# Two output projections as 2x2 block products with seven products in place of eight

## The chip, the cores and the metric

The kernel runs on one NeuronCore of one Trainium2 chip, as one program. The metric is the device time of one execution in microseconds; the times shown are of three executions.

## The reference

Two encoder layers are computed for 64 sample tokens (of a running stream) and 512 prompt tokens, 576 in all, with a model width of 2048. Layer A is attention over a band of chunks with 16 heads of 128; layer B is latent attention with 16 heads. Both end in the same way, and that end is what is changed:

```python
y = x + (jax.nn.silu(g) * o) @ w_out      # w_out: 2048 x 2048, once in a_prompt/a_sample, once in b_prompt/b_sample
```

`x` is the layer's input (for layer B the `y` of layer A), `o` the heads' outputs side by side (2048 columns), `g` a gate of the same width. Layer B begins with `rmsnorm(x) @ w_b_in`. All of it is float32.

## The kernel before, in words

All activations are kept transposed: features on the 128 partitions, the 576 tokens on the free axis, so a 2048x576 matrix is 16 tiles of 128x576. Weights are the stationary operand. A float32 product is three float32r passes: each operand is split into a rounded part `hi` (a cast on ACT) and the rest `lo` (a subtraction on DVE), and TensorE adds hi*hi, hi*lo and lo*hi into one PSUM sum.

An output projection goes over 16 output tiles `m`. For each, `proj` takes 16 tiles of input features (`o2`, hi and lo, which stay in SBUF), three passes each, with the 576 tokens in two halves of 288 that lie in two PSUM banks: 96 matmuls a tile. `wload` brings a quarter of a tile's weights (128x512, 256 KB) by the SP queue into one of three raw buffers and splits it into one of five pairs of hi and lo buffers; `Weights` does that three quarters ahead. The first two output tiles (`both`) are merged with the last heads of attention: their matmuls fill the time in which PE would wait for a head. Tile by tile DVE then adds the residual (L681 in layer A, L1039 in layer B). In layer A the sum `x1` goes to DRAM (`x1d`, by the POOL queue; layer B reads it again as its residual) and is split in SBUF at once, with the factor per feature of layer B's norm (`split_g`, L686), into `h`, the operand of layer B's input products (`lat`). Its squares are summed for the norm (L265).

In layer B attention has no room for the heads' outputs in SBUF; 14 of 16 go to DRAM (`od`) and are read back and split in time (`reload`); the last two are split from SBUF.

The order of PE's instructions is the program's: class `Order` merges streams (attention, gates, output) into one fixed list, in which a stream waits for a time, a PSUM buffer or a condition. The other engines and queues are ordered by the framework's scheduler from priorities and dependences, each again as one fixed list that its engine goes through in order; it also sets the semaphore waits. PSUM has a tag `mm` of two tiles of two banks, and one tile each of `st` and `x`.

Of the kernel before, what the change touches and what calls it, by code (L numbers as in the profile page):

```python
# [12 lines left out]
F32 = mybir.dt.float32  # L13
F32R = mybir.dt.float32r
# [75 lines left out]
class Weights:  # L90
    """Tiles of weights in the order of their use, each loaded and split `ahead` of it."""
# [24 lines left out]
def encoder(tc, xT, wa_in, wa_out, wb_in, wuq, wuk, wuqr, wuv, wb_out, kcT, vc, ckvcT, krcT, gains, rtab,  # L116
# [38 lines left out]
    def matmul(out, lhs, rhs, start, stop):  # L155
# [5 lines left out]
        nc.tensor.matmul(out, lhs, rhs, start=start, stop=stop)  # L161
# [95 lines left out]

    def square_sum(acc, src, tp, w, first, name):
        """acc += src**2, elementwise."""
# [7 lines left out]
    def col_sums(sq, tp, w, ones_ap, name, wait=2.0):  # L267
        """st[:, c, :w/2] = column sums of sq on every partition; and two buffers that are free then."""
# [12 lines left out]
    def halves(src, tp, w, name):  # L281
        """The column sums of src**2: the squares of both halves of the partitions are added first."""
# [57 lines left out]
    def gate(ps, rs, dst, tp, name):  # L340
        """dst = silu(ps * rs), the sigmoid as exp(min(g, 0) - ln(1 + exp(-|g|)))."""
# [9 lines left out]
    def softmax(s_ps, w, nb, pp, name):  # L351
        """Rows of exp(-(s + nb)) over their sum, s the negated scores."""
# [96 lines left out]
    # ------------------------------------------------------------------ layer A: input  # L449
# [42 lines left out]
    def head_a(hd):  # L492
        """The projections of a head; what follows each goes its own way."""
# [67 lines left out]
        def bias():  # L561
            """By relative position, less its value at far keys; negated."""
# [84 lines left out]
    wo = Weights(wload, two_first(parts_of(wa_out, range(KT), "wao")), 3)  # L647
# [10 lines left out]
    # ------------------------------------------------------------------ layer A: output  # L658
    close(g_at)
    close(g_o)  # L660
    g_x1, x1p = pool("x1", side="right")
    g_ao, aop = pool("aout", side="right")

    def tpo(tag, dt, name):
        return aop.tile([P, N], dt, tag=tag, bufs=2 if tag in ("xr", "x1", "s1") else 1, name=name)

    h = []
    acc = tpo("acc", F32, "lnb_acc")

    def out_a():  # L670
        for m in range(KT):
            xr = tpo("xr", F32, f"xr{m}")
            nc.sync.dma_start(xr, xT[m * P:(m + 1) * P, :])
            if m < 2:
                ps = first[m]
            else:
                yield "mm"
                ps = ps_of("mm", f"ao{m}")
                yield from proj(ps, wo, o2, N)
            x1 = tpo("x1", F32, f"x1_{m}")  # L680
            V.tensor_tensor(out=two(x1), in0=ps[:, :, :288], in1=two(xr), op=ALU.add)  # L681
            od_.give("mm", L_M)
            nc.gpsimd.dma_start(x1d[m * P:(m + 1) * P, :], x1)
            hi = x1p.tile([P, N], F32R, tag="x1", bufs=32, name=f"bh{m}")
            lo = x1p.tile([P, N], F32R, tag="x1", bufs=32, name=f"bl{m}")
            split_g(x1, gn[:, G_LNB + m:G_LNB + m + 1], hi, lo)  # L686
            h.append((hi, lo))
            square_sum(acc, x1, tpo, N, m == 0, f"lnb{m}")
# [5 lines left out]
    # ------------------------------------------------------------------ layer B: latents  # L694
# [6 lines left out]
    close(g_ao)  # L701
    g_l, lp = pool("lat")
# [4 lines left out]

    cq = [(lp.tile([P, N], F32R, name=f"cqh{m}"), lp.tile([P, N], F32R, name=f"cql{m}")) for m in range(4)]
# [20 lines left out]
    def rope(x, name):  # L729
        """x rotated in place; x: two stacked sets of 64 features."""  # L730
# [44 lines left out]
    def rotary_key(ps):  # L775
        """Twice: rows 64.. repeat rows ..63."""
# [26 lines left out]
    def queries():  # L803
        """Of the heads, rotary ones two heads at a time; to DRAM."""
# [47 lines left out]
    # ------------------------------------------------------------------ layer B: heads  # L852
# [23 lines left out]
    def prepare():  # L876
        """Keys of the heads, values of two at a time."""
# [16 lines left out]
    def values_of(pr, w):  # L894
        """Of two heads, tokens on partitions."""
# [37 lines left out]
    def fetch():  # L933
        """The heads' queries."""
# [17 lines left out]
    def attend(hd):  # L952
# [25 lines left out]
        if hd < H - DIRECT:  # L978
            nc.gpsimd.dma_start(od[hd * P:(hd + 1) * P, :], sg)
        else:  # L980
# [25 lines left out]
    wo = Weights(wload, two_first(parts_of(wb_out, range(KT), "wbo")), 3)  # L1006
    first = []

    def out_first():
        """The first tiles of the output, as far as heads are done."""  # L1010
# [14 lines left out]
    # ------------------------------------------------------------------ layer B: output  # L1025
    g_bo, bo = pool("bout")

    def out_b():
        for m in range(KT):
            xr = bo.tile([P, N], F32, tag="xr", bufs=2, name=f"bxr{m}")  # L1030
            nc.sync.dma_start(xr, x1d[m * P:(m + 1) * P, :])
            if m < 2:
                ps = first[m]
            else:
                yield "mm"
                ps = ps_of("mm", f"bo{m}")
                yield from proj(ps, wo, o2, N)
            y = bo.tile([P, N], F32, tag="y", bufs=2, name=f"by{m}")
            V.tensor_tensor(out=two(y), in0=ps[:, :, :288], in1=two(xr), op=ALU.add)  # L1039
            od_.give("mm", L_M)  # L1040
            nc.gpsimd.dma_start(yT[m * P:(m + 1) * P, :], y)
# [99 lines left out]
```

## Time and profile before

| what | us |
|---|---|
| time, median of three executions | 2042.68 (2042.22 to 2042.9) |
| span of the profiled execution (its own time is recorded only as this span) | 2040.6 |
| TensorE (PE) busy | 2021.8 |
| VectorE (DVE) busy | 1182.7 |
| ScalarE (ACT) busy | 1037.9 |
| GpSimd (POOL) busy | 73.5 |
| layer A, output tiles 2 to 15: from, to | 974, 1153 |
| layer B, output tiles 2 to 15: from, to | 1856, 2035 |

The page gives busy times of one execution; a matmul's own duration overlaps with the next one's, so the time that one takes is read from the distance of two starts or from a piece of the chain, not from its mean duration. The same holds for DVE, where successive instructions overlap by some 0.09 us. PE's line says that it hardly ever rests. What another engine's time means is to be read stage by stage, from what PE waits for there.

### The profile page before, as it was taken

To read this page: it belongs to the slowest core of one execution; us is meant where nothing else is said; L and a number is where in the kernel's file an instruction comes from. 1 tells how busy PE (TensorE), PEld (TensorE's weight loads), DVE (VectorE), ACT (ScalarE), POOL (GpSimd) and SP (SyncE) were. 2 spreads that over 40 slices of the span, in tenths; PEclk is the share of its full clock that TensorE was granted. 3 is DMA by queue.
4 is the path that set the end of the run, shared out by engine and by line. 5 is a ranking of instruction groups with operands and counts; after the bars stand their busy time and mean duration, and the time that the engine had idled before them with its cause. 6 is when DMAs were issued, how large, how long until landed. Compare 5 with 4: busy or idle time off the path is not lost.

```text
span 2040.6 us, 37379 instructions
## 1 busy us (share of the span) xinstructions
PE 2021.8 (99%) x14980; PEld 2002.9 (98%) x14980; DVE 1182.7 (58%) x2295; ACT 1037.9 (51%) x1898; POOL 73.5 (4%) x139
## 2 busy tenths in 40 slices
PE   8999999999999999999999999999999999999998
PEld 8999999999999999999999999999999999999998
DVE  7665555555555555556433448887776766673221
ACT  6654444544454445455333338886765656572111
POOL 0000000000000000000000000000000000000000
PEclk9999999999999999999999999999999999999999
DMA  7333333333333332323444425563223322354442
GB/s 212 85 84 94 90 85 90 82 86 89 86 94 89 86 90 77 85 81 91 145 129 130 122 75 145 160 165 119 77 82 92 88 85 88 83 150 138 129 129 76
DMA packets 116621, 213.33 MB, mean 105 GB/s; under 512 B 13728, under 2 KB 28720, under 8 KB 116448
## 3 DMA queue, kind: packets, MB, share of 16 engines
q1 hardware_dynamic: 104752, 171.78, 31.0%
q0 software_dynamic: 11696, 39.17, 5.5%
q8 instruction: 117, 1.92, 0.4%
q14 instruction: 56, 0.46, 0.1%
HBM read 174.48 MB, written 33.77 MB: 102 GB/s over the span
## 4 chain that ended last, share of the span: by engine, by line
PE 89%; issue 8%; DVE 1%; ACT 1%; POOL 0%; DMA 0%; POOLq 0%; DVEq 0%; ACTq 0%
PE ao L161 10%; PE g L161 8%; PE lat L161 7%; PE u L161 3%; PE a2p L161 3%; PE bo L161 3%; PE a7p L161 3%; PE a15p L161 3%; PE a13p L161 3%; PE a10p L161 3%; PE a8p L161 3%; PE a12p L161 3%; PE a14p L161 3%; PE a6p L161 3%; PE a5p L161 3%
## 5 line engine op out<-in xcount | busy, mean ns | idle before, releaser
L201 DVE TENSOR_TENSOR wa_2l<-wa_2r,wa_2h 128x512 fp32r<-128x512 f32 x61 | 42.2, 691 | 92.2 <-ACT wa_2h L200 92.2
L200 ACT CAST wa_2h<-wa_2r 128x512 fp32r<-128x512 f32 x61 | 37.7, 619 | 103.7 <-PE a2p L161 10.1
L200 ACT CAST wa_0h<-wa_0r 128x512 fp32r<-128x512 f32 x61 | 37.8, 619 | 61.1 <-PE a2p L161 4.3
L201 DVE TENSOR_TENSOR wa_3l<-wa_3r,wa_3h 128x512 fp32r<-128x512 f32 x61 | 42.2, 692 | 43.5 <-ACT wa_3h L200 42.0
L200 ACT CAST wa_3h<-wa_3r 128x512 fp32r<-128x512 f32 x61 | 37.7, 618 | 50.8 <-PE a2p L161 4.5
L201 DVE TENSOR_TENSOR wa_0l<-wa_0r,wa_0h 128x512 fp32r<-128x512 f32 x61 | 41.9, 687 | 17.6 <-ACT wa_0h L200 17.6
L200 ACT CAST wa_1h<-wa_1r 128x512 fp32r<-128x512 f32 x61 | 37.8, 620 | 25.0 <-PE a0pg L161 2.6
L201 DVE TENSOR_TENSOR wa_1l<-wa_1r,wa_1h 128x512 fp32r<-128x512 f32 x61 | 41.8, 686 | 11.8 <-ACT wa_1h L200 11.7
L1039 DVE TENSOR_TENSOR by<-bo,bxr 128x576 f32<-128x576 f32 x16 | 12.1, 757 | 43.5 <-PE bo L161 43.5
L681 DVE TENSOR_TENSOR x<-ao,xr 128x576 f32<-128x576 f32 x16 | 12.1, 758 | 33.1 <-PE ao L161 33.1
L201 DVE TENSOR_TENSOR wao_3l<-wao_3r,wao_3h 128x512 fp32r<-128x512 f32 x16 | 11.1, 691 | 34.1 <-ACT wao_3h L200 34.1
L201 DVE TENSOR_TENSOR wbo_2l<-wbo_2r,wbo_2h 128x512 fp32r<-128x512 f32 x16 | 11.0, 690 | 32.9 <-ACT wbo_2h L200 32.9
L201 DVE TENSOR_TENSOR wbo_3l<-wbo_3r,wbo_3h 128x512 fp32r<-128x512 f32 x16 | 11.0, 690 | 32.7 <-ACT wbo_3h L200 32.6
L200 ACT CAST wao_3h<-wao_3r 128x512 fp32r<-128x512 f32 x16 | 9.9, 620 | 39.2 <-PE ao L161 39.2
L201 DVE TENSOR_TENSOR wao_2l<-wao_2r,wao_2h 128x512 fp32r<-128x512 f32 x16 | 11.1, 691 | 32.5 <-ACT wao_2h L200 32.3
L200 ACT CAST wbo_3h<-wbo_3r 128x512 fp32r<-128x512 f32 x16 | 9.9, 621 | 37.8 <-PE bo L161 37.7
L161 PE MATMUL u<-cqh,wq_0h 128*128 128x288 f32 x128 | 27.6, 297 | 0.5 <-ACT q6raw L336 0.3
L201 DVE TENSOR_TENSOR wb_1l<-wb_1r,wb_1h 128x512 fp32r<-128x512 f32 x25 | 17.2, 688 | 18.6 <-ACT wb_1h L200 18.6
L201 DVE TENSOR_TENSOR wbo_1l<-wbo_1r,wbo_1h 128x512 fp32r<-128x512 f32 x16 | 11.0, 690 | 29.1 <-ACT wbo_1h L200 29.1
L161 PE MATMUL ao<-oh,wao_1h 128*128 128x288 f32 x128 | 27.6, 297 | 0.0
L161 PE MATMUL ao<-oh,wao_0h 128*128 128x288 f32 x128 | 27.5, 296 | 0.0
L161 PE MATMUL bo<-boh,wbo_2h 128*128 128x288 f32 x128 | 27.5, 296 | 0.0
(5236 smaller groups left out, 7717.5 us busy)
## 6 DMA issues: line engine op xcount, KB each, us to landing
wa_0r<-wa_in SPq DMA_DIRECT2D x61, 256.0 KB, 2.9
wa_1r<-wa_in SPq DMA_DIRECT2D x61, 256.0 KB, 2.9
wa_2r<-wa_in SPq DMA_DIRECT2D x61, 256.0 KB, 2.9
wa_3r<-wa_in SPq DMA_DIRECT2D x61, 256.0 KB, 2.9
wb_0r<-wb_in SPq DMA_DIRECT2D x25, 256.0 KB, 3.0
wb_1r<-wb_in SPq DMA_DIRECT2D x25, 256.0 KB, 3.0
wb_2r<-wb_in SPq DMA_DIRECT2D x25, 256.0 KB, 3.0
wb_3r<-wb_in SPq DMA_DIRECT2D x25, 256.0 KB, 2.9
```

The costliest lines, as they stand in the source:

```text
L161: nc.tensor.matmul(out, lhs, rhs, start=start, stop=stop)
L200: ACT.copy(hi, src)
L201: V.tensor_tensor(out=lo, in0=src, in1=hi.bitcast(F32), op=ALU.subtract)
L681: V.tensor_tensor(out=two(x1), in0=ps[:, :, :288], in1=two(xr), op=ALU.add)
L1039: V.tensor_tensor(out=two(y), in0=ps[:, :, :288], in1=two(xr), op=ALU.add)
```

## The change

The first two output tiles of each layer are made as before. The other 14 are made as seven pairs. A pair of output tiles (256 features) by 576 tokens is cut into four quarters (a tile, a half of the tokens), and the 2048 input features into two halves of eight tiles: a 2x2 block product of 2x2 blocks, which takes eight block products of 24 matmuls. The new code takes seven, in Winograd's form of Strassen's scheme, over sums and differences of blocks:

- `block_operands` builds the four combined operands (numbers 4 to 7; 1 to 3 are parts of `o2`) once a layer, from the float32 outputs of the heads, in place, and splits them; number 4 is put where one half of `o2` was.
- `block_weights` loads a pair's eight raw blocks and builds its sums S0 and S1 and differences, on DVE (L324, 327, 330, 334), then splits 14 of them.
- `block_pairs` does the products. Those of five numbers accumulate on sums already in PSUM: a tile of two banks takes all products but number 2. After each product DVE adds what the bank holds to the output (L391).

In layer A the raw weights take the 16 buffers of the heads' outputs (`oA`). `x1` goes only to DRAM; when the projection's buffers are free, 16 loads (L855) bring it back for `split_g`. In layer B all 16 heads go to `od`, and after the heads' buffers are free 16 loads (`bf`, L1196) bring them back for `block_operands`; the raw weights then take the same 16 buffers.

```diff
+    def block_operands(o, o2, pool, name):
+        L, R = slice(0, 288), slice(288, 576)
+        ...                                  # X[1], X[2], X[3]: halves of o2
+        def put(p, j, src):
+            if p == 4:
+                hi, lo = [x[:, R] for x in o2[j]]
+            else:
+                hi = pool.tile([P, 288], F32R, tag="T", bufs=48, name=f"{name}T{p}h{j}")
+                lo = pool.tile([P, 288], F32R, tag="T", bufs=48, name=f"{name}T{p}l{j}")
+            split(src, hi, lo)
+            X[p].append((hi, lo))
+        for j in range(8):
+            V.tensor_tensor(out=o[j][:, L], in0=o[j][:, R], in1=o[j][:, L], op=sub)
+            put(5, j, o[j][:, L])
+        for j in range(8):
+            a, b = o[j], o[j + 8]
+            V.tensor_tensor(out=a[:, R], in0=b[:, R], in1=a[:, R], op=sub)
+            V.tensor_tensor(out=b[:, R], in0=b[:, R], in1=a[:, L], op=sub)
+            put(6, j, b[:, R])
+        ...                                  # 7 from o[j][:, R]; 4 from o[j+8][:, L] - o[j+8][:, R]
+    def block_weights(w2d, pairs, order, raw_tile, name):
+        ...
+                    elif p == 5:
+                        S[c] = raw_tile(f"{n_}s{c}")
+                        V.tensor_tensor(out=S[c], in0=block(1, 0, c), in1=block(1, 1, c), op=ALU.add)
+                    elif p == 6:
+                        V.tensor_tensor(out=S[c], in0=S[c], in1=block(0, 0, c), op=ALU.subtract)
+        ...
+                    split(src, hi, lo)
+                    yield hi, lo
+    def block_pairs(w2d, X, pairs, raw_tile, residual, out_tile, done, name):
+        order = [(1, 2, 5, 6, 3, 7, 4) if n == 0 else (1, 5, 6, 3, 7, 2, 4) for n in range(len(pairs))]
+        ws = Ahead(block_weights(w2d, pairs, order, raw_tile, name), WHL - 2)
+        for (m1, m2), seq in zip(pairs, order):
+            ...
+            ps = ps_of("mm", n_ + "ac")
+            bank = {1: ps[:, 0, :288], 5: ps[:, 1, :288]}
+            bank[6] = bank[7] = bank[4] = bank[1]
+            bank[3] = bank[5]
+            for p in seq:
+                if p == 2:
+                    bank[2] = ps_of("x", n_ + "b")[:, :288]
+                for c in range(2):
+                    hi, lo = ws.get()
+                    for j in range(4):
+                        ...
+                        begins = p in (1, 2, 5) and c == 0 and j == 0
+                        matmul(bank[p], hi[:, s], xh, begins, False, skip_group_check=True)
+                        matmul(bank[p], hi[:, s], xl, False, False, skip_group_check=True)
+                        matmul(bank[p], lo[:, s], xh, False, ends, skip_group_check=True)
+                with tc.high_priority():
+                    y, h_, add = ...
+                    V.tensor_tensor(out=y[:, h_], in0=bank[p], in1=add[:, h_], op=ALU.add)
@@ layer A
+    X = block_operands(oA, o2, Tp, "ao")
+    def raw_a(name):
+        return op_.tile([P, WH], F32, tag="o", bufs=16, name=name)
+    def done_a(m, x1):
+        nc.gpsimd.dma_start(x1d[m * P:(m + 1) * P, :], x1)
+        square_sum(acc, x1, tpo, N, m == 0, f"lnb{m}")
-            hi = x1p.tile([P, N], F32R, tag="x1", bufs=32, name=f"bh{m}")
-            lo = x1p.tile([P, N], F32R, tag="x1", bufs=32, name=f"bl{m}")
-            split_g(x1, gn[:, G_LNB + m:G_LNB + m + 1], hi, lo)
@@ layer B, latents
+    for m in range(KT):
+        x1 = tpl("raw", F32, f"bx{m}")
+        nc.sync.dma_start(x1, x1d[m * P:(m + 1) * P, :])
+        ...
+        split_g(x1, gn[:, G_LNB + m:G_LNB + m + 1], hi, lo)
@@ layer B, heads
-        if hd < H - DIRECT:
-            nc.gpsimd.dma_start(od[hd * P:(hd + 1) * P, :], sg)
-        else:
+        nc.gpsimd.dma_start(od[hd * P:(hd + 1) * P, :], sg)
+        if hd >= H - DIRECT:
@@ layer B, output
+    for kt in range(KT):
+        oB.append(bo.tile([P, N], F32, tag="o", bufs=16, name=f"bf{kt}"))
+        nc.sync.dma_start(oB[kt], od[kt * P:(kt + 1) * P, :])
+    X = block_operands(oB, o2, bo, "bo")
```

Three places in the engines' lists follow. First PE in layer A, where the sum that is made changes: before from output tile 8 (`ao8`) to tile 9, after from product 5 to product 6 of the pair of tiles 8 and 9 (`ao8p5...` and `ao8p6...` are the weights, `aoT5...` and `aoT6...` the combined operands). In brackets stands what a matmul waits for. Before:

```order
L161 MATMUL ao8_12074<-oh15_11203,wao8_3h_12076 128x288 x2
L161 MATMUL ao8_12074<-ol15_11204,wao8_3h_12076 128x288 x2
L161 MATMUL ao8_12074<-oh15_11203,wao8_3l_12077 128x288 x2
L161 MATMUL ao9_12207<-oh0_10861,wao9_0h_12106 128x288 [waits DVE_49,Activation_49]
L161 MATMUL ao9_12207<-oh0_10861,wao9_0h_12106 128x288
L161 MATMUL ao9_12207<-ol0_10862,wao9_0h_12106 128x288 x2
```

After:

```order
L164 MATMUL ao8ac_12238<-aoT5h7_11265,ao8p51h_12245 128x288
L164 MATMUL ao8ac_12238<-aoT5l7_11266,ao8p51h_12245 128x288
L164 MATMUL ao8ac_12238<-aoT5h7_11265,ao8p51l_12246 128x288
L164 MATMUL ao8ac_12238<-aoT6h0_11271,ao8p60h_12262 128x288 [waits DVE_49,Activation_49]
L164 MATMUL ao8ac_12238<-aoT6l0_11272,ao8p60h_12262 128x288
L164 MATMUL ao8ac_12238<-aoT6h0_11271,ao8p60l_12263 128x288
```

Before, the sum changes to another tile (`ao8`, `ao9`), and the wait on DVE is for an addition to a tile that was finished 96 matmuls earlier. After, both products are in one tile, `ao8ac`, in its two banks, and the count of DVE that product 6 waits for is that of the addition `x1_9<-ao8ac,xr9` (L391), which waits for product 5's last matmul.

The second place is DVE at the end of layer A's last head, from its last multiplication (`a15sg`) on. `ol` are lo parts of the heads' outputs, `wao` and `ao2p` weights. Before:

```order
L427 TENSOR_TENSOR a15sg_10850<-a15sg_10850,a15o3_11085 128x512
L201 TENSOR_TENSOR ol15_11204<-a15sg_10850,oh15_11203 128x576
L201 TENSOR_TENSOR wao2_1l_11181<-wao2_1r_11179,wao2_1h_11180 128x512
L201 TENSOR_TENSOR wao2_2l_11193<-wao2_2r_11191,wao2_2h_11192 128x512
L681 TENSOR_TENSOR x1_0_11254<-ao0_10859,xr0_11252 128x576
```

After, the first rows and the last:

```order
L567 TENSOR_TENSOR a15sg_10850<-a15sg_10850,a15o3_11085 128x512
L204 TENSOR_TENSOR aoT5l0_11231<-a0sg_769,aoT5h0_11230 128x288
L290 TENSOR_TENSOR a4sg_3547<-a12sg_8867,a4sg_3547 128x288
L204 TENSOR_TENSOR aoT5l1_11236<-a1sg_1540,aoT5h1_11235 128x288
L204 TENSOR_TENSOR ol15_11186<-a15sg_10850,oh15_11185 128x576
...
L204 TENSOR_TENSOR aoT7l7_11346<-a7sg_5542,aoT7h7_11345 128x288
L204 TENSOR_TENSOR ol7_11031<-a15sg_10850,oh7_11030 128x288
L825 TENSOR_TENSOR x1_1_11385<-ao1_10860,xr1_11383 128x576
L204 TENSOR_TENSOR ao2p10l_11401<-ao2r2_0_11398,ao2p10h_11400 128x512
```

The weights of output tile 2 stood two rows behind the multiplication; now 51 rows (48 of 288 columns, 3 of 576) stand between it and the first weights of the pair of tiles 2 and 3.

The third place is SP's queue of loads in layer B, behind the last head read back for the first two tiles (`bo13`). Before:

```order
L993 DMA bo13_21354<-od_70 128x576
L214 DMA wbo2_0r_21510<-wb_out 128x512
L214 DMA wbo2_1r_21576<-wb_out 128x512
L214 DMA wbo2_2r_21588<-wb_out 128x512
L214 DMA wbo2_3r_21654<-wb_out 128x512
L1031 DMA bxr0_21641<-x1d_69 128x576
```

After:

```order
L1144 DMA bo13_21640<-od_70 128x576
L1196 DMA bf0_21910<-od_70 128x576
L1196 DMA bf1_21912<-od_70 128x576
...
L1196 DMA bf14_21938<-od_70 128x576
L1196 DMA bf15_21940<-od_70 128x576
L1184 DMA bxr0_22086<-x1d_69 128x576
L1184 DMA bxr1_22091<-x1d_69 128x576
L309 DMA bo2r2_0_22103<-wb_out 128x512
```

The weights of tile 2 stood right behind `bo13`; now the 16 loads of the heads' outputs and two of the residual go first. The load of `bf1` takes the buffer of the last head's output and waits for that one's write to `od`.

## Rows read from the trace of the kernel before

**Rows 1.** The page: span, and busy time of each engine (share of the span, instructions).
```profile
span 2040.6 us, 37379 instructions
...
PE 2021.8 (99%) x14980; PEld 2002.9 (98%) x14980; DVE 1182.7 (58%) x2295; ACT 1037.9 (51%) x1898; POOL 73.5 (4%) x139
```

**Rows 2.** Chain of waits, two stretches: start us, us, what.
```profile
961.18 192.00 PE ao L161 x1440
...
1518.36 6.48 PE v3v L161 x54
```

**Rows 3.** By stretch: us, busy PE, PEld, DVE, ACT, POOL; clock, DMA share, GB/s.
```profile
974.00:1153.00 179.00, 179.00 (x1344) 179.00 (x1344) 69.52 (x99) 54.08 (x86) 7.58 (x15) 1.00 0.46 132
1856.00:2035.00 179.00, 179.00 (x1344) 178.90 (x1342) 45.30 (x66) 32.05 (x52) 7.58 (x14) 1.00 0.41 122
7.00:30.00 23.00, 22.68 (x153) 22.34 (x154) 18.56 (x28) 18.00 (x30) 0.00 (x0) 1.00 0.86 266
25.00:30.00 5.00, 5.00 (x39) 5.00 (x39) 2.86 (x6) 3.14 (x6) 0.00 (x0) 1.00 0.92 303
```

**Rows 4.** PE, timeline: start us, us, instruction xcount [idle before <-what ended it].
```profile
86.78 0.42 PE L161 MATMUL a1p<-hh,wa_2l 128*128 128x288 f32 x2
88.20 0.50 PE L161 MATMUL a10st<-a10s,ones 128*128 128x288 f32 x2 [1.00 <-DVE a01sq L325]
88.54 0.42 PE L161 MATMUL a1p<-hh,wa_3h 128*128 128x288 f32 x2
...
961.01 0.42 PE L161 MATMUL ao<-oh,wao_2h 128*128 128x288 f32 x2
...
1153.02 0.42 PE L161 MATMUL lat<-bh,wb_0h 128*128 128x288 f32 x2
...
1846.98 0.43 PE L161 MATMUL bo<-boh,wbo_2h 128*128 128x288 f32 x2
...
2034.71 0.42 PE L161 MATMUL bo<-boh,wbo_3l 128*128 128x288 f32 x2
```

**Rows 5.** DVE, timeline of the same places.
```profile
87.31 0.75 DVE L325 SCALAR_TENSOR_TENSOR a01sq<-a01st,a01sq 128x576 f32<-128x576 f32 x1
...
936.21 0.67 DVE L201 TENSOR_TENSOR wao_1l<-wao_1r,wao_1h 128x512 fp32r<-128x512 f32 x1
936.81 0.74 DVE L201 TENSOR_TENSOR ol<-a4sg,oh 128x576 fp32r<-128x576 f32 x1
...
941.36 0.75 DVE L201 TENSOR_TENSOR ol<-a8sg,oh 128x576 fp32r<-128x576 f32 x1
942.02 0.75 DVE L201 TENSOR_TENSOR ol<-a9sg,oh 128x576 fp32r<-128x576 f32 x1
...
961.22 0.69 DVE L427 TENSOR_TENSOR a15sg<-a15sg,a15o 128x512 f32<-128x512 f32 x1 [0.84 <-PE a15o L161]
...
1847.18 0.69 DVE L427 TENSOR_TENSOR g15sg<-g15sg,b15o 128x512 f32<-128x512 f32 x1 [3.82 <-PE b15o L161]
...
2035.17 0.76 DVE L1039 TENSOR_TENSOR by<-bo,bxr 128x576 f32<-128x576 f32 x1 [12.04 <-PE bo L161]
```

**Rows 6.** Groups, DVE, forms apart: instruction xcount | busy, mean ns | idle before.
```profile
L527 DVE TENSOR_TENSOR a0vt<-a0pv,rs 128x288 f32<-128x288 f32 x2 | 0.8, 451 | 0.0
```

**Rows 7.** DMA issues: out<-in, queue, KB each, median us to landing.
```profile
x1d<-x POOLq DMA_DIRECT2D x16, 288.0 KB, 3.9
...
wao_0r<-wa_out SPq DMA_DIRECT2D x16, 256.0 KB, 2.9
...
od<-g8sg POOLq DMA_DIRECT2D x1, 288.0 KB, 2.4
```

**Rows 8.** PE, timeline of the kernel's start.
```profile
8.81 0.68 PE L161 MATMUL a0pq<-hh,wa_0l 128*128 128x288 f32 x2
...
12.02 0.43 PE L161 MATMUL a0pg<-hh,wa_0h 128*128 128x288 f32 x2
```

More of the change, by code (lines that the diff above doesn't have):

```diff
@@ L153, in two, with matmul @@
         return ap.rearrange("p (c n) -> p c n", c=2)
-    def matmul(out, lhs, rhs, start, stop):
+    def matmul(out, lhs, rhs, start, stop, **kw):
         n = rhs.shape[-1]
@@ L160, in matmul @@
             od_.now += 4 * (n / 2.4 + 2) / 1e3
-        nc.tensor.matmul(out, lhs, rhs, start=start, stop=stop)
+        nc.tensor.matmul(out, lhs, rhs, start=start, stop=stop, **kw)
     def transpose(out, in_):
@@ new lines, in block_weights, with load, block @@
+    def block_weights(w2d, pairs, order, raw_tile, name):
+        for (m1, m2), seq in zip(pairs, order):
+            n_ = f"{name}{m1}"
+            got, S = {}, {}
+            def load(m, part):
+                r = raw_tile(f"{n_}r{m}_{part}")
+                nc.sync.dma_start(r, w2d[m * P:(m + 1) * P, part * WH:(part + 1) * WH])
+                return r
+            def block(i, k, c):
+                key = i, k, c
+                if key not in got:
+                    got[key] = load((m1, m2)[i], 2 * k + c)
+                return got[key]
+            for p in seq:
+                for c in range(2):
+                    if p == 1:
+                        src = block(0, 0, c)
+                    elif p == 5:
+                        S[c] = raw_tile(f"{n_}s{c}")
+                        V.tensor_tensor(out=S[c], in0=block(1, 0, c), in1=block(1, 1, c), op=ALU.add)
+                        src = S[c]
+                    elif p == 6:
+                        V.tensor_tensor(out=S[c], in0=S[c], in1=block(0, 0, c), op=ALU.subtract)
+                        src = S[c]
+                    elif p == 3:
+                        V.tensor_tensor(out=S[c], in0=block(0, 1, c), in1=S[c], op=ALU.subtract)
+                        src = S[c]
+                    elif p == 7:
+                        src = block(1, 0, c)
+                        V.tensor_tensor(out=src, in0=block(0, 0, c), in1=src, op=ALU.subtract)
+                    elif p == 2:
+                        src = block(0, 1, c)
+                    else:
+                        src = block(1, 1, c)
+                    hi = wp.tile([P, WH], F32R, tag="whi", bufs=WHL, name=f"{n_}p{p}{c}h")
+                    lo = wp.tile([P, WH], F32R, tag="wlo", bufs=WHL, name=f"{n_}p{p}{c}l")
+                    split(src, hi, lo)
+                    yield hi, lo
@@ new lines, in encoder, with __init__, fill, get @@
+    class Ahead:
+        def __init__(self, gen, n):
+            self.gen, self.n, self.got = gen, n, []
+        def fill(self, n):
+            while len(self.got) < n:
+                x = next(self.gen, None)
+                if x is None:
+                    break
+                self.got.append(x)
+        def get(self):
+            self.fill(self.n + 1)
+            return self.got.pop(0)
+    def block_pairs(w2d, X, pairs, raw_tile, residual, out_tile, done, name):
+        L, R = slice(0, 288), slice(288, 576)
+        order = [(1, 2, 5, 6, 3, 7, 4) if n == 0 else (1, 5, 6, 3, 7, 2, 4) for n in range(len(pairs))]
+        ws = Ahead(block_weights(w2d, pairs, order, raw_tile, name), WHL - 2)
+        for (m1, m2), seq in zip(pairs, order):
+            n_ = f"{name}{m1}"
+            x1, x2 = residual(m1), residual(m2)
+            y1, y2 = out_tile(m1), out_tile(m2)
+            yield "mm"
+            ps = ps_of("mm", n_ + "ac")
+            bank = {1: ps[:, 0, :288], 5: ps[:, 1, :288]}
+            bank[6] = bank[7] = bank[4] = bank[1]
+            bank[3] = bank[5]
+            for p in seq:
+                if p == 2:
+                    yield "x"
+                    bank[2] = ps_of("x", n_ + "b")[:, :288]
+                for c in range(2):
+                    hi, lo = ws.get()
+                    for j in range(4):
+                        s = slice(j * P, (j + 1) * P)
+                        xh, xl = X[p][4 * c + j]
+                        ends = c == 1 and j == 3
+                        begins = p in (1, 2, 5) and c == 0 and j == 0
+                        matmul(bank[p], hi[:, s], xh, begins, False, skip_group_check=True)
+                        matmul(bank[p], hi[:, s], xl, False, False, skip_group_check=True)
+                        matmul(bank[p], lo[:, s], xh, False, ends, skip_group_check=True)
+                        yield None
+                with tc.high_priority():
+                    y, h_, add = {1: (y1, L, x1), 5: (y2, R, x2), 6: (y1, R, x1), 3: (y1, R, y1), 7: (y2, R, y2),
+                                  2: (y1, L, y1), 4: (y2, L, x2)}[p]
+                    V.tensor_tensor(out=y[:, h_], in0=bank[p], in1=add[:, h_], op=ALU.add)
+                if p == 2:
+                    od_.give("x", L_M)
+            od_.give("mm", L_M)
+            done(m1, y1)
+            done(m2, y2)
@@ L645, in heads_a @@
                 o2[j] = hi, lo
-    wo = Weights(wload, two_first(parts_of(wa_out, range(KT), "wao")), 3)
+    wo = Weights(wload, two_first(parts_of(wa_out, range(2), "wao")), 3)
     first = []
@@ L701, in encoder @@
     close(g_ao)
+    close(g_T)
+    close(g_o)
+    g_x1, x1p = pool("x1", side="right")
     g_l, lp = pool("lat")
@@ L977, in attend @@
         sg = gates[hd][0]
-        if hd < H - DIRECT:
-            nc.gpsimd.dma_start(od[hd * P:(hd + 1) * P, :], sg)
-        else:
+        nc.gpsimd.dma_start(od[hd * P:(hd + 1) * P, :], sg)
+        if hd >= H - DIRECT:
             yield lambda: flag["gates"] == KT and o2[hd - 1] is not None
@@ L1004, in heads_in @@
         yield since[kt] + 4.0
-    wo = Weights(wload, two_first(parts_of(wb_out, range(KT), "wbo")), 3)
+    wo = Weights(wload, two_first(parts_of(wb_out, range(2), "wbo")), 3)
     first = []
@@ L1026, in encoder, with raw_b, residual_b, out_tile_b @@
     g_bo, bo = pool("bout")
-    def out_b():
[L1029 to L1039, printed above, removed]
+    def raw_b(name):
+        return bo.tile([P, WH], F32, tag="o", bufs=16, name=name)
+    def residual_b(m):
+        xr = bo.tile([P, N], F32, tag="xr", bufs=2, name=f"bxr{m}")
+        nc.sync.dma_start(xr, x1d[m * P:(m + 1) * P, :])
+        return xr
+    def out_tile_b(m):
+        return bo.tile([P, N], F32, tag="y", bufs=2, name=f"by{m}")
+    def done_b(m, y):
+        nc.gpsimd.dma_start(yT[m * P:(m + 1) * P, :], y)
+    oB = []
+    for kt in range(KT):
+        oB.append(bo.tile([P, N], F32, tag="o", bufs=16, name=f"bf{kt}"))
+        nc.sync.dma_start(oB[kt], od[kt * P:(kt + 1) * P, :])
+    X = block_operands(oB, o2, bo, "bo")
+    def out_b():
+        for m in range(2):
+            xr = residual_b(m)
+            y = out_tile_b(m)
+            V.tensor_tensor(out=two(y), in0=first[m][:, :, :288], in1=two(xr), op=ALU.add)
             od_.give("mm", L_M)
-            nc.gpsimd.dma_start(yT[m * P:(m + 1) * P, :], y)
+            done_b(m, y)
+        yield from block_pairs(wb_out, X, [(m, m + 1) for m in range(2, KT, 2)], raw_b, residual_b, out_tile_b,
+                               done_b, "bo")
     od_.spawn(5, out_b())
```

45 lines of the change are left out of this document (29 added, 16 removed).

## The prediction, made before the changed kernel had run

> **What bounds the kernel now.** The first view is the page's busy line: TensorE (PE) is busy for 2021.8 of the 2040.6 us span, and every other engine is far below that [rows 1]. So what the change makes of PE's time is the answer, and other engines count only where PE comes to wait for them. The second is the chain of waits: from 961.18 us one unbroken piece of 192.00 us, 1440 matmuls of layer A's output projection, 133.3 ns for one with 288 columns [rows 2]. The third is the table by stretch: in the 179 us in which layer A's tiles 2 to 15 are made PE has no idle time, DVE is busy 69.5 us; in layer B it is the same, with DVE at 45.3 [rows 3]. These two stretches (14 tiles of 96 matmuls, 1344 each) are what the change rewrites. The span lies 2.1 us below the median of 2042.68, and I add terms to the median, as if the same 2.1 us stay around it.
>
> **What is saved.** A pair of tiles has eight 128x1024 by 1024x288 block products of 24 matmuls, 3.2 us each, 25.6 us in all. Seven are left: 22.4. Seven pairs in two layers make 14 x 3.2 = 44.8 us saved, if a matmul that accumulates in one bank takes as long as one that changes banks: 54 matmuls of 256 columns in one bank took 6.48 us, 120 ns each [rows 2], which is 13 ns less than for 288 columns, in step with the columns. So I take no loss there.
>
> **What a product now waits for.** This is the term that decides. All sums of a pair except product 2's lie in one tile of two banks (`ac`), used in turn. In the order of PE the first matmul of each product on it has a wait on DVE, and its count is that of the add (L391) that reads the sum of the product just before, though that one lies in the other bank. It is so in 56 places: four in each pair. (The fifth wait of a pair has a product of 3.2 us in between and is met by then.) Before, two tiles took turns and 96 matmuls lay between. Behind the waiting matmul is all of PE's order, and nothing else can go. One hand-over, from rows: last matmul's slot to the start of the add, 0.20 us (bo: 2034.71 + 0.27 = 2034.98, the add at 2035.17; b15o: PE goes on at 1846.98, DVE starts at 1847.18) [rows 4, 5]; the add of 288 columns from PSUM 0.45 [rows 6]; from its end to PE's first matmul 0.14, and 0.07 more that the first two take (DVE a01sq ends at 88.06, PE starts at 88.20 and the next is at 88.54, 0.34 for two instead of 0.27) [rows 4, 5]. Sum 0.86, say 0.85. Bounds: 0.70 (0.20 + 0.37 + 0.14, an add at its streaming rate, below) and 1.25 (one 128x512 instruction of 0.60 still running as the sum gets ready, in two cases of three). 56 x 0.85 = 47.6, from 39 to 70.
>
> The trace shows two engines at work on different PSUM tiles at once everywhere, but no two on two banks of one tile. The Trainium skill, "PSUM — Partial Sum Buffer", section "PSUM bank collisions raise a hardware error", says that PSUM has to be guarded by bank and quadrant: only accesses of the same bank have to be kept apart. If the waits went by that rule, each would be met one product earlier and the 47.6 us would be nothing; that is rival 1. The order shows that they don't.
>
> Is DVE free when an add is due? In a pair it has in layer A 22 instructions of 512 columns, 7 adds and 2 of 576: 22 x 0.60 + 7 x 0.45 + 2 x 0.67 = 17.7 us (B: 16.4) [spacings in rows 5] of some 25.8. So it mostly stands at the add before PE gets there. Once a pair it doesn't: the second half of the next pair's weight sum (L324) waits for a load of 2.9 us [rows 7] whose buffer an L327 frees 1.9 us after product 4 begins; it lands 1.8 us after that product's end, three more instructions and the add of product 1 follow, some 0.35 late. 14 x 0.35 = 4.9 us. All waits: 52.5.
>
> **Three starts.** Each leaves PE empty.
> (1) Layer A's first pair. After the last head's multiply (961.22, 0.60 long) DVE has 51 instructions before the first lo part of the new weights: 48 of 288 columns and 3 of 576. Spacing is 0.60 for 512 columns and 0.67 for 576 [rows 5], 1.04 ns each, so 0.37 for 288: 48 x 0.37 + 3 x 0.67 = 19.8; with 0.8 for ACT's cast of the last head and 0.7 for the lo part, 983.3. The 16 operand instructions ahead of that multiply fit in idle time that DVE has there. PE has 96 matmuls of the first two tiles left at 961.01: to 973.8. Gap 9.5 us (7.5 if ACT is hidden and fewer are left, 13.5 at the 0.45 duration of one).
> (2) A to B. Before, layer B's first matmul follows on the last one at 1153.02 [rows 4], since x1 was split from SBUF tile by tile. Now 16 tiles come back from DRAM, the first issued behind a weight load that waits for the last add, some 1.8 us after the last matmul. With 3 weight loads, cos, sin and two writes 23 transfers of 0.29 MB have to pass; at the 266 to 303 GB/s that loads alone reach [rows 3] that is 22 to 25 us. Layer B's first tile (13.6 us of PE before) ends 25.5 us after the last matmul in place of 13.6: gap 12 (8 where DVE's 16 lo parts set it, 16 with 3.9 us [rows 7] of write latency ahead of the last).
> (3) Layer B's first pair. All heads' outputs are read back. The second of the 16 loads takes the buffer of head 15's output: it waits for that one's write, issued at about 1847.9 (multiply from 1847.18 [rows 5]) and landing 2.4 to 3.9 us later [rows 7]. 15 loads of 0.295 MB at 280 GB/s, 1.05 us each, bring the last at 1868 to 1870. Behind it DVE has 28 instructions of 288 columns and 2 of 576, 11.7 us: the first lo part is there at 1882. PE has 66 matmuls left at 1846.98, to 1855.8. Gap 26 us (21 with quick transfers and half of the casts hidden, 31 at 0.45 a piece).
> After a gap PE is slow. At the kernel's start 14 matmuls from 8.81 to 12.02 took 229 ns each, then 133 [rows 8]: half the rate, though the stretch's column says 1.00 [rows 3]. Some 18 of them cost 18 x 0.107 = 1.9 us. After an idle 1.15 us (87.05 to 88.20) the rate was whole [rows 4], so the 56 short waits cost no clock. I take two such restarts, 3.8 us (0 to 5.7). The Trainium skill, "TensorE: Matmul & The Clock Gate", section "What's actually happening", agrees with the start: throttled is the default state, and activity releases it. That a gap in mid-kernel puts it back no row here shows.
> The last add covers half a tile: -0.3.
>
> **Sum.** -44.8 + 47.6 + 4.9 + 9.5 + 12 + 26 + 3.8 - 0.3 = +58.7: 2101 us. All low ends: -44.8 + 39 + 36.5 - 0.3 = +30, 2073. All high ends: -44.8 + 70 + 4.9 + 60.5 + 5.7 = +96, 2139.
>
> **Rivals.**
> Rival 1, not slower: PE doesn't stand still between products, because the count in the wait is reached one product earlier than I read it (as the rule on banks would have it). Its place is the 56 product starts and its price 0. Then the starts alone stand against the saving. At their low ends it is 2042.7 - 44.8 + 36.5 - 0.3 = 2034; as I took them, 2049. It is not slower where the three gaps with the restarts stay under 49 us. For it: the two banks in turn. Against it: the counts in the order.
> Rival 2: DVE is behind at every add, by one instruction of 0.60 us, since each pair's sums, lo parts and adds form one line in which the lo parts wait for PE to free buffers. 56 x 0.60 = 34 more: 2135. For it: 17.7 us of work with waits on loads and ACT between. Against: 8 us of spare time a pair.
> Rival 3: only the gaps fail to come, since loads and operands get ready under the first two tiles: 2101 - 51 = 2050, for which DVE would need those 20 us twice over in 961 to 974; rows speak against it.
>
> **Chances.** Forecast .69 (its own range 2073 to 2125), rival 1 .13, rival 2 .13, rival 3 .05. The range takes in the forecast's and rival 2's time up to 2138 and stops at 2060, short of most of rival 1. A difference of 0.2%, 4 us, is about what a measurement can tell from none. Of rival 1 .04 falls to faster and .04 within that bound, with .01 of rival 3; the rest is slower: .91.
>
> **What would show it.** A PE chain broken into pieces of 3.2 us in both output stages, with idle time of about 0.85 us ended by DVE L391, 56 in all; pairs of 25.8 to 26.2 us instead of 22.4. An idle PE of 8 to 13 us before layer A's first pair, ended by DVE L204; about 12 spread over layer B's first tile, ended by the split of the reloaded tiles; 21 to 31 in layer B, again by L204. Rows at half rate behind these. I am wrong if products follow on each other without idle time (rival 1), or if idle time before a product is ended by L204 or an ACT cast rather than by the add (rival 2), or if the clock is lost in the short waits.

## The result and the profile after

The changed kernel takes 2113.67 us (2112.47 to 2114.16, four runs), the one before 2042.78 beside it: 1.0347 times, 95% interval 1.0332 to 1.0361. It is 71 us slower. The forecast was 2101, with a range from 2060 to 2138.

The page of the profile after, for [rows 1]:

```profile
span 2110.7 us, 37527 instructions
...
PE 2001.0 (95%) x14644; PEld 1968.2 (93%) x14644; DVE 1375.2 (65%) x2689; ACT 1112.7 (53%) x2046; POOL 74.4 (4%) x141
...
PEclk9999999999999999999999999999999999998999
```

PE has the 336 matmuls less that the scheme saves, but its busy time falls by 20.8 us only, and the span grows by 70.1. So PE now stands still for 90.9 us more than before. The waits of PE show where (who waits for whom: us in all, times, longest):

```profile
PE bo2ac L164 <- DVE by L1203: 23.2, 1, 23.2
PE lat L164 <- ACT bh L208: 9.7, 1, 9.7
PE ao2ac L164 <- DVE x L825: 7.1, 1, 7.1
...
PE bo6ac L164 <- DVE by L391: 2.0, 1, 2.0
...
PE ao2ac L164 <- DVE ao2p10l L204: 1.8, 1, 1.8
...
PE ao8ac L164 <- DVE x L391: 1.4, 1, 1.4
...
PE ao8ac L164 <- ACT ao8p20h L203: 0.6, 1, 0.6
```

There are three long waits, at the three starts, and a long list of short ones on the tiles `ac`. One of the short ones, on PE and then on DVE (product 6 of tiles 8 and 9 ends, product 3 begins), for [rows 4, 5]:

```profile
1076.71 0.29 PE L164 MATMUL ao8ac<-aoT6h,ao8p61l 128*128 128x288 f32 x1
1077.65 0.37 PE L164 MATMUL ao8ac<-oh,ao8p30h 128*128 128x288 f32 x1 [0.64 <-ACT ao8p20h L203]
1077.86 0.29 PE L164 MATMUL ao8ac<-ol,ao8p30h 128*128 128x288 f32 x1
```

```profile
1076.03 0.69 DVE L204 TENSOR_TENSOR ao8p71l<-ao8r,ao8p71h 128x512 fp32r<-128x512 f32 x1 [1.80 <-ACT ao8p71h L203]
1077.04 0.46 DVE L391 TENSOR_TENSOR x<-ao8ac,xr 128x288 f32<-128x288 f32 x1 [0.33 <-PE ao8ac L164]
```

Product 6's last slot ends at 1076.84, the add starts 0.20 later and ends at 1077.50, PE starts 0.15 after that, and the first matmul takes 0.21 us until the next one starts instead of 0.13. The profile names ACT's cast `ao8p20h` as what ended the wait. That cast makes weights for product 2, which product 3 doesn't read; it is only the last event seen before PE went on. What a wait is for has to be checked against what the instruction reads and waits on; here the time of the add's end and the order agree, the name doesn't. Of the 56 waits between products the profile names an ACT cast for 40 and the add (L391) for 16.

Two pairs and a stretch after two of the starts, by stretch, for [rows 3] (columns as there):

```profile
1011.88:1038.52 26.64, 23.28 (x171) 22.46 (x170) 18.84 (x32) 9.94 (x16) 1.08 (x2) 1.00 0.43 124
1998.18:2025.10 26.92, 23.21 (x170) 22.40 (x169) 17.34 (x30) 8.68 (x14) 1.08 (x2) 1.00 0.44 123
984.00:988.00 4.00, 4.00 (x17) 4.00 (x18) 3.52 (x6) 0.62 (x1) 0.00 (x0) 0.50 0.91 217
1975.00:1978.00 3.00, 3.00 (x13) 3.00 (x14) 0.83 (x2) 0.17 (x1) 0.00 (x0) 0.50 0.33 87
```

Behind the first pair of a layer a pair takes 26.1 to 27.1 us, and tiles 6 and 7 of layer B 28.7 (before, two tiles took 25.6). Its seven products take 22.4, the rest is mostly waits. In the third row the granted clock is 0.50, the 1.2 GHz level, behind the empty start of layer A; the fourth lies behind a short wait in tiles 6 and 7 of layer B.

### The profile page after: what moved, and what is told of

The parts are those of the page before. It is cut to its first block, busy times and chain, and to the rows that moved or that the text cites. A ratio compares the mean times of both kernels' runs of the same rounds, so it can differ in the third digit from the quotient of the medians.

```text
span 2110.7 us, 37527 instructions
## 1 busy us (share of the span) xinstructions
PE 2001.0 (95%) x14644; PEld 1968.2 (93%) x14644; DVE 1375.2 (65%) x2689; ACT 1112.7 (53%) x2046; POOL 74.4 (4%) x141
## 5 line engine op out<-in xcount | busy, mean ns | idle before, releaser
L204 DVE TENSOR_TENSOR wa_2l<-wa_2r,wa_2h 128x512 fp32r<-128x512 f32 x61 | 42.2, 691 | 92.2 <-ACT wa_2h L203 92.2
L204 DVE TENSOR_TENSOR wa_3l<-wa_3r,wa_3h 128x512 fp32r<-128x512 f32 x61 | 42.2, 692 | 44.1 <-ACT wa_3h L203 42.5
L204 DVE TENSOR_TENSOR wa_0l<-wa_0r,wa_0h 128x512 fp32r<-128x512 f32 x61 | 41.9, 687 | 17.0 <-ACT wa_0h L203 17.0
L204 DVE TENSOR_TENSOR wa_1l<-wa_1r,wa_1h 128x512 fp32r<-128x512 f32 x61 | 41.8, 686 | 11.5 <-ACT wa_1h L203 11.5
L164 PE MATMUL lat<-bh,wb_0h 128*128 128x288 f32 x88 | 20.0, 311 | 9.7 <-ACT bh L208 9.7
L204 DVE TENSOR_TENSOR wb_1l<-wb_1r,wb_1h 128x512 fp32r<-128x512 f32 x25 | 17.2, 688 | 16.0 <-ACT wb_1h L203 15.9
L164 PE MATMUL u<-cqh,wq_0l 128*128 128x288 f32 x128 | 27.4, 296 | 0.0
L164 PE MATMUL u<-cql,wq_0h 128*128 128x288 f32 x128 | 27.3, 295 | 0.0
L204 DVE TENSOR_TENSOR wb_3l<-wb_3r,wb_3h 128x512 fp32r<-128x512 f32 x25 | 17.2, 687 | 15.1 <-ACT wb_3h L203 15.0
L203 ACT CAST wb_1h<-wb_1r 128x512 fp32r<-128x512 f32 x25 | 15.5, 619 | 18.8 <-PE lat L164 10.0
L164 PE MATMUL g<-bh,wb_1h 128*128 128x288 f32 x112 | 24.3, 298 | 0.0
L164 PE MATMUL g<-bh,wb_0h 128*128 128x288 f32 x112 | 24.3, 298 | 0.0
L164 PE MATMUL g<-bh,wb_2h 128*128 128x288 f32 x112 | 24.3, 298 | 0.0
L164 PE MATMUL g<-bh,wb_3h 128*128 128x288 f32 x112 | 24.2, 298 | 0.0
L164 PE MATMUL g<-bh,wb_0l 128*128 128x288 f32 x112 | 24.0, 296 | 0.0
```

The source lines that it names most:

```text
L164: nc.tensor.matmul(out, lhs, rhs, start=start, stop=stop, **kw)
```

## The experiments

**Two PSUM tiles.** The second sum of a pair moves to the tile `st`; all else stays.

```diff
-            ps = ps_of("mm", n_ + "ac")
-            bank = {1: ps[:, 0, :288], 5: ps[:, 1, :288]}
+            bank = {1: ps_of("mm", n_ + "ac")[:, 0, :288]}
+            yield "st"
+            bank[5] = ps_of("st", n_ + "a5")[:, 0, :288]
```

> The changed kernel, only that the second sum of a pair (products 5 and 3) lies in the PSUM tile `st` instead of in the second bank of the same tile. Theory (PE waits for the add of the product before because both banks are one tile): of the 56 waits of 0.8 us and more only the two in front of product 4 of each first pair stay; the others add up to 54 us with 4 us of slow first matmuls behind them, so 2113.7 - 57 = about 2056 us, pairs of 22.4 to 23 us. Rival (DVE is what bounds a pair, the add is only where it shows): PE's idle time moves to the lo parts and casts of the weights, pairs stay at 25 us or more, at most 25 us are gained: 2088 or slower.

Measured: 2054.31 us, 59 less than the changed kernel (1.0057 of before, 1.0042 to 1.0072). The pairs, by stretch, and the place that stood above (product 6, then 3, now of tiles 6 and 7) on PE:

```profile
1031.42:1053.69 22.27, 22.27 (x170) 22.27 (x169) 18.39 (x32) 9.94 (x16) 1.08 (x2) 1.00 0.49 148
```

```profile
1040.82 0.29 PE L164 MATMUL ao6ac<-aoT6h,ao6p61l 128*128 128x288 f32 x1
1040.95 0.30 PE L164 MATMUL ao6a<-oh,ao6p30h 128*128 128x288 f32 x1
```

PE is busy for all of the 22.27 us, with the same 32 DVE instructions as in the slow pair. So DVE was not what bound a pair: the waits were made by two sums in one tile, and the rival named above, that DVE bounds a pair, is out. Of the 56 waits the two in front of product 4 of each first pair are left, as expected.

**No sums of weights.** Products 5, 6, 3 and 7 take raw blocks of weights.

```diff
-                        S[c] = raw_tile(f"{n_}s{c}")
-                        V.tensor_tensor(out=S[c], in0=block(1, 0, c), in1=block(1, 1, c), op=ALU.add)
-                        src = S[c]
+                        src = block(1, 0, c)
...
```

> The changed kernel without the sums and differences of weight blocks (products 5, 6, 3 and 7 take raw blocks; what is computed is not the projection). 112 DVE instructions of 0.60 us go. Theory: the hand-over of 0.81 us stays in all 56 places, and only the longer waits in front of product 5 (1.1 to 2.2 us, where the sum for the next pair and its load stand ahead of the add) fall to 0.81: 10 us less, with the slow matmuls behind the longest of them 11 to 12, so about 2102. Rival (DVE's load as such makes the waits): all 56 get shorter, 25 us or more, 2088 or faster. Second rival (the long waits come from loads or casts): under 4 us, 2110.

Measured: 2099.71 us (1.0277, 1.0262 to 1.0293), 14 less, where 11 to 12 were expected. In both layers all 56 waits are 0.80 or 0.81 us from end to start; the 1.1 to 2.2 in front of product 5 are gone. Product 5 of tiles 8 and 9, with the add (L386 here) that it waits for:

```profile
1066.93 0.46 DVE L386 TENSOR_TENSOR x<-ao8ac,xr 128x288 f32<-128x288 f32 x1 [0.36 <-PE ao8ac L164]
...
1067.54 0.37 PE L164 MATMUL ao8ac<-aoT5h,ao8p50h 128*128 128x288 f32 x1 [0.64 <-ACT ao8p30h L203]
```

So the hand-over stands by itself, and what the sums bring, DVE's work and the loads that it waits for, adds to it at one place in a pair. This run takes out both and doesn't tell them apart.

**x1 through DRAM, nothing else.** The kernel before; `split_g` in the output loop goes, and the 16 loads `bx` with their split come in layer B, as in the change.

> The kernel before, only that layer A's sum x1 goes through DRAM alone and its 16 tiles are loaded and split again for layer B; no block products. Theory: the start of layer B costs what it costs in the changed kernel, 9.9 us of empty PE and about 5 us of slow matmuls and waits for tiles: 2042.8 + 15 = 2058 (2054 to 2061). Rival (the changed kernel's boundary is slow because of the block products in front of it): under 8 us, 2050 or faster.

Measured: 2050.87 us, +8.5 (1.0040, 1.0026 to 1.0054), between theory and rival, and much less than in the changed kernel. The start of layer B on PE in this run, then in the changed kernel:

```profile
1153.38 0.43 PE L161 MATMUL ao<-oh,wao_3l 128*128 128x288 f32 x2
1157.55 0.85 PE L161 MATMUL lat<-bh,wb_0h 128*128 128x288 f32 x2 [3.74 <-ACT bh L205]
```

```profile
1170.58 0.29 PE L164 MATMUL ao14ac<-oh,ao14p41l 128*128 128x288 f32 x1
1180.56 0.85 PE L164 MATMUL lat<-bh,wb_0h 128*128 128x288 f32 x2 [9.70 <-ACT bh L208]
```

And the loads on SP's queue, with ACT's splits of them, in the same sequence:

```profile
1151.79 0.33 SPq L214 DMA_DIRECT2D wb_1r<-wb_in  x1
1152.21 3.31 SPq L706 DMA_DIRECT2D bx<-x1d  x7
...
1156.72 2.90 ACT L205 ACTIVATE bh<-bx,gn 128x576 fp32r<-128x576 f32 x4
```

```profile
1172.19 0.33 SPq L217 DMA_DIRECT2D wb_2r<-wb_in  x1
1172.62 4.43 SPq L855 DMA_DIRECT2D bx<-x1d  x7
...
1179.74 5.28 ACT L208 ACTIVATE bh<-bx,gn 128x576 fp32r<-128x576 f32 x7 [6.10 <-DMA bx<-x1d]
```

Without block products the loads go out 1.4 us ahead of the end of layer A's last matmul (1153.64); in the changed kernel 1.9 us behind it (1170.71), since one more weight load (`wb_2r`) stands in front and waits for a buffer. In both runs seven loads go out at once, for seven buffers; the first lands 4.4 us after its issue here and 7.1 in the changed kernel. PE's gap is 3.9 us here and 9.85 there. Of the 5.9 between them 3.3 are the place in SP's list and 2.7 the slower landing. The DMA engines are busier there until that load lands (mean share 0.93 against 0.81); which transfers slow it was not separated. Up to the end of layer B's first tile (100 matmuls) the round trip alone costs 7.8 us, in the changed kernel 14.8.

**Layer B alone.** Layer A's projection and the hand-over as before.

> The changed kernel with layer A's output projection and the hand-over to layer B as before; only layer B has block products. Theory: layer B's part alone by its stage in the changed trace (216.2 us from the end of the first two tiles against 179.2): 2042.8 + 37 = 2080 (2077 to 2083). Rival (the layers' costs depend on each other, for instance through a lower clock later): off by more than 4 us.

Measured: 2078.53 us (1.0176, 1.0161 to 1.0192), as expected from its stage alone. The rest of the 71 us, layer A's projection with the hand-over, did not run by itself; nothing here speaks for the layers changing each other's cost.

**Layer B alone, two PSUM tiles.** The edit of the first run and the one above together.

> Block products in layer B alone (layer A as before), with the two sums of a pair in two PSUM tiles. Theory: of 2078.5 us layer B's waits go, 28.1 us of idle PE, 2 us of slow first matmuls behind them and 1.5 us at half rate in one product: about 2047 (2044 to 2050). What is left over the kernel before is then the start (27 us) less the saving (22.4). Rival: in layer B, where weights and loads come later than in A, the pairs get bound by DVE once the add is out of the way: 2055 or slower.

Measured: 2047.74 us (1.0028, 1.0016 to 1.0039), as expected. With whole pairs of 22.3 us the start of layer B's first pair, 27 us, is what keeps it slower than before.

**Four old tiles, operands beside them.** Of layer B's output, tiles 2 and 3 too are made the old way; reloads and operands come step by step between their matmuls, operand 4 behind the pair's products. The two sums keep their two tiles.

```diff
+                for _ in proj(ps, wo, o2, N):
+                    load_o()
+                    if k >= 4:
+                        next(early, None)
+                    k += 1
+                    yield None
...
+        yield from block_pairs(wb_out, X, [(m, m + 1) for m in range(4, KT, 2)], ..., late)
```

> As the run before (layer B alone, two PSUM tiles), but four output tiles are made the old way and six pairs by block products; the reloads of the heads and the building of the operands are given out step by step beside tiles 2 and 3 (25.6 us of PE). Theory (the start costs because PE has nothing to do meanwhile): one pair's saving, 3.2 us, is lost, and of the start's 27 us at most 3 stay: 2047 + 3.2 - 25 = about 2025. Rival (the reloads and operands take DVE and the queue that tiles 2 and 3 need, and the wait only moves into them): 8 us or more stay, 2031 or slower.

Measured: 2031.00 us (0.9946, 0.9930 to 0.9963), faster than before. The rival's mark of 2031 was just met: product 5 of the first pair took 7.7 us with a wait of 2.94 in it, and products 1 and 6 each a microsecond more than 3.2. Product 5 waited for weights whose sum waited for the pair's last raw loads. SP's queue around those loads, and what its loads waited for in 1870 to 1890:

```profile
1877.53 3.67 SPq L311 DMA_DIRECT2D bo4r<-wb_out  x6
1886.27 0.33 SPq L1178 DMA_DIRECT2D bxr<-x1d  x1
1886.71 0.84 SPq L311 DMA_DIRECT2D bo4r<-wb_out  x2
```

```profile
SPq L1178 <- DVE by L1213: 8.2, 2, 5.0
SPq L311 <- DVE bol L204: 7.5, 4, 4.9
```

The two last weight loads stand behind a load of the residual (`bxr`), which waits 5.0 us for a buffer that the addition to tile 3 (L1213, ended at 1886.24) frees, and go out 0.44 us after it. So the buffers that operand building frees, which the next runs are aimed at, were not all that held them.

**The same in both layers**, and then with layer B's 16 loads of x1 on POOL's queue.

> The same in both layers: two PSUM tiles, four old tiles, operands built beside tiles 2 and 3. Against the run before layer A adds a saving of 6 x 3.2 = 19.2 us and the way of x1 through DRAM, 13 to 15 us: theory 2025 - 19.2 + 14 + 1 = 2021 (2018 to 2025). Rival: in layer A too a start of over 5 us stays, 2026 or slower.

Measured: 2029.92 us (0.9941, 0.9926 to 0.9955), not the 2021 hoped for. Layer A's start is gone (its first product follows the old tiles after one matmul's 0.14 us). But its 19.2 us go to layer B's start, whose first tile ends 16.1 us later behind layer A's last matmul than in the kernel before (10.9 us of it empty PE, then slow matmuls), and to 2.2 us in front of product 4.

> As the run before, only that the 16 loads of x1 for layer B are issued by POOL's queue instead of SP's, where they stand behind a weight load that waits for the last add. Theory (the first load is late by its place in SP's queue, and slow since twelve are issued at once): the first comes 1 us earlier and lands in 3 to 4 us instead of 7, 3 to 5 us gained: 2017. Rival (the boundary is bound by the 16 transfers and the splits): under 1.5 us.

Measured: 2033.16 us (0.9949, 0.9930 to 0.9968; four runs from 2026.39 to 2034.63): no gain in the whole time. At the place itself the first load went out 1.5 us after layer A's last matmul instead of 2.3 and landed after 6.1 us instead of 7.8; layer B's first tile ended 1.7 us sooner behind layer A's last matmul (28.0 for 29.7), just over the rival's mark and short of the theory's 3 to 5. PE's idle time there was 9.5 us instead of 10.9; ACT, on which the splits stand, this time waited 5.5 us for a small load (`krc`) first, 0.9 us longer than for the first tile of x1. The profiled execution lost it again elsewhere: in front of product 4 of layer A's first pair PE waited 3.2 us in place of 2.2 and then ran some 14 matmuls at half rate.

**Sums apart.** As the four-tile versions, with the sums of weights in the old path's raw buffers and operands earlier; first in layer B alone, then in both.

```diff
-                        S[c] = raw_tile(f"{n_}s{c}")
+                        S[c] = wp.tile([P, WH], F32, tag="wraw", bufs=WRAW, name=f"{n_}s{c}")
```

> The run with four old tiles and six pairs in layer B alone, with the sums of weights in the three raw buffers of the old path, so that two more buffers of the 16 are free for the first pair's loads, operands begun two steps earlier, and operand 4 finished within two products. Theory (what was left of the start, 7.7 us in the first pair's products 1, 5, 6 and 7, comes from the pair's last raw loads waiting for buffers that operand building frees late): 3 to 5 us less, about 2027. Rival (DVE's work as such is too long for the 25.6 us of tiles 2 and 3): under 1.5 us less, 2029.5 or slower.

Measured: 2031.56 us (0.9942, 0.9925 to 0.9958): no change, the theory fell. Product 5 of the first pair came down from 7.7 to 4.5 us, but products 6 and 3 went up to 5.1 and 4.4, and the heads ahead ended later. Of the 3.4 us by which the first pair begins later, 1.35 arise at the kernel's start and the rest in layer B up to its heads, where the text of the two kernels is the same; from there to the second pair it is 28.6 us against 30.2. So the stage gained 1.6 us, about half of the least that the theory asked for. DVE is busy for 24.0 of the 25.8 us ahead of the first pair and for 26.3 of the 28.2 in it: that fits the rival, that its work is too much for this place, though no run takes work from DVE here to show it.

> The same in both layers. Theory: as the run with both layers (2030), less what layer B gains, about 2026; layer A's gain of 19.2 us is still eaten by the 14 to 16 us that the way of x1 through DRAM costs.

Measured: 2023.25 us (0.9903, 0.9889 to 0.9918), the fastest of all, 20 us under the kernel before and 90 under the changed one. Against the version before it without the sums apart layer A's wait in front of product 4 fell from 2.2 to 0.8 us, and layer B's first matmul came 3.7 us sooner. Between the two profiled executions lie 5.9 us: 3.7 up to there, 0.4 from there to layer B's first pair, and the 1.9 by which that pair is shorter. What moved the start of layer B was not separated.

## Why the prediction was right

Its terms, each beside what the trace of the changed kernel shows:

| term | predicted | measured |
|---|---|---|
| saved products | -44.8 | -46 (22.27 us a pair in the run with two tiles, against 179.0 / 7 = 25.57) |
| 56 waits with slow first matmuls | 47.6 + 4.9 = 52.5 | 55.7 idle + 4.5 slow (56 x 0.08) + 1.6 at half rate in one product = 61.8 |
| start of layer A, with half rate | 9.5 + 1.9 | 11.8 |
| start of layer B, with half rate | 12 | 14.8 |
| start of layer B's first pair, with half rate | 26 + 1.9 | 27.6 |
| sum, with -0.3 for the tail | +58.7 | +69.7 (spans: +70.1) |

The step on the product waits held: their number (56), place, and size for 44 of them, 0.81 us idle and 0.08 for the slow first matmul, 0.89 against 0.85. It was read from the order, since no row of before showed two sums in one tile, and the run with two tiles shows it by 59 us. Rival 1, each wait met one product earlier, was priced at 2049; with the sums in two tiles, where that is so, the kernel comes to 2054. The Trainium skill, "PSUM — Partial Sum Buffer", section "PSUM bank collisions raise a hardware error", asks for a guard by bank (and quadrant); no run here guards two banks of one tile apart, so its rule stays untried, and the program's waits, which go by whole tiles, decided.

The time alone would have proved little: the range takes in rival 2's 2135 as well, and 2113.67 lies between it and 2101. The sum was 12 us short, most of it in the waits (9.3) and at layer B's start (2.8). What tells the rivals apart is where PE stands and the two runs with two tiles and without sums.

The mis-sized term is the wait in front of product 5. I took 0.35 us of lateness once a pair, from a load that lands late. Measured are 1.25 to 1.64 us of idle time in layer A and 1.12 to 2.17 in layer B, 20.0 us for the twelve (the two first pairs have none there), where I had 14. DVE in layer A and then in layer B at one of them:

```profile
1067.04 0.69 DVE L324 TENSOR_TENSOR ao10s<-ao10r,ao10r 128x512 f32<-128x512 f32 x1 [0.34 <-DMA ao10r<-wa_out]
1067.65 0.75 DVE L405 TENSOR_TENSOR lnb_acc<-lnb_acc,lnb7sq 128x576 f32<-128x576 f32 x1
1068.32 0.69 DVE L204 TENSOR_TENSOR ao8p61l<-ao8s,ao8p61h 128x512 fp32r<-128x512 f32 x1
1068.92 0.45 DVE L391 TENSOR_TENSOR x<-ao8ac,xr 128x288 f32<-128x288 f32 x1
```

```profile
2000.27 0.69 DVE L324 TENSOR_TENSOR bo10s<-bo10r,bo10r 128x512 f32<-128x512 f32 x1 [0.58 <-DMA bo10r<-wb_out]
2000.87 0.68 DVE L330 TENSOR_TENSOR bo8s<-bo8r,bo8s 128x512 f32<-128x512 f32 x1
2001.48 0.69 DVE L204 TENSOR_TENSOR bo8p61l<-bo8s,bo8p61h 128x512 fp32r<-128x512 f32 x1
2002.08 0.68 DVE L334 TENSOR_TENSOR bo10r<-bo10r,bo10r 128x512 f32<-128x512 f32 x1
2002.68 0.45 DVE L391 TENSOR_TENSOR by<-bo8ac,bxr 128x288 f32<-128x288 f32 x1
```

Product 1 ended at 2001.34. The load is late, as said. Counted from L324, which waits for it, layer A's list has the three instructions ahead of the add that the prediction counts, and layer B's has four, with L330 and L334 in place of L405; the add in layer B starts 1.14 us after it could. Layer A's list was used for both layers, and in layer A too the wait came out longer than the 1.2 priced. Rival 2 (late at every add) is out: it is one add of seven. Its sign in the prediction was an idle time ended by L204 or an ACT cast, and by the profile's names 40 of the 56 waits would bear it; only the times and what a matmul reads show that the add ended them.

The start of layer A came out by its steps: the new weights' first lo part was forecast for 983.3 (its terms add up to 983.1) and ended at 983.75. In the third, head 15's last matmul stands 33.5 us later than in the kernel before (1880.48 for 1846.98, where the output's own go on), so the forecast 1882 becomes 1915.5; that lo part ended at 1914.1, and PE stood empty for 23.2 us and, one matmul later, 0.7; with more matmuls at half rate than priced the sum still came out. The second start was 2.8 us too cheap, and its mechanism was another: I had the rate of 23 transfers set the end of layer B's first tile, 25.5 us after the last matmul, with the idle time spread over the tile. Measured is 28.4, with 9.85 us of idle time in one piece ahead of the tile, 1.9 until the first load goes out and 7.1 until it lands, and half rate behind, where I had none. Rival 3, that loads and operands get ready beside the first two tiles, fell with the three gaps.

The clock: behind layer A's start the profile shows half rate from 983.81 to 988.3, about 4.5 us, with 0.50 granted. I had counted two such restarts, which the table puts at the two first pairs; the trace has one behind each of the three starts and one behind a short wait, where I had none.

## What to carry to other kernels

A saving on a saturated engine is worth what the new order lets through: look up, at each new hand-over, which instruction's count the engine waits for, since here the waits were set by whole tiles, which made two banks of one tile one resource; give each sum that is read while another grows a tile of its own. Then price the empty time at the start of each new stage, from the list of what stands between the last old and the first new operand: here three starts cost 54 us, more than the 46 that the scheme saves. Look there for the load that waits in a queue, since it holds all that stand behind it (`wb_2r`, `bxr`). Work that only has to be done in time is best handed out between the instructions that the engine still has (in layer B, four old tiles instead of two gave up one pair's saving of 3.3 us, and the kernel still came down from 2047.74 to 2031.00).

## What the runs showed of the hardware

The pause that brings the clock down has no one length in these runs. Before product 5 of tiles 6 and 7 in layer B PE was idle for 2.17 us, and 14 matmuls then ran at half rate (the 1975 to 1978 row above, granted 0.50, 1.2 GHz); before the same product of the pairs from tile 10 and tile 12 it was 2.02 and 2.07 us, in the run with layer B alone 2.26 (tiles 4 and 5) and in the version with both layers 2.22 us (product 4 of layer A's first pair), each time with full rate behind. The other 55 waits, of 0.8 to 2.1 us, left the clock at 1.00. The Trainium skill, "TensorE: Matmul & The Clock Gate", section "What's actually happening", says that the default is throttled and activity releases it; the starts agree with that (0.50 in 984 to 988, full rate from 988.46), and which short pause counts no run here settles.
